# Two-megabyte weight transfers in slots of double size, with a new order of the first loads and of four routing copies

## The chip, the cores and the metric

The kernel runs on one core of a Trainium2 chip as one launch. The metric is device time in microseconds (us). Three runs of the kernel before gave a median of 1549.14 us (1548.66 to 1551.61).

## The reference

Two transformer blocks run one after the other on 256 tokens of width 1024, in float32:

```python
x = first_block(...)    # norm, w_in, pool mixer + attention, w_out; cross attention on mem; conv FFN
x = second_block(...)   # modulation by w_mod; latent attention over x and ctx; Fourier mix; w_out; experts

# the experts' part, the longest
logits = h @ w_router + b_router                 # 32 experts, the best 4 of each token
g = minimum(xb @ w_gate[e] + b_gate[e], 7)
u = clip(xb @ w_up[e] + b_up[e], -7, 7)
act = g * sigmoid(1.702 * g) * (u + 1)
y += gate * (act @ w_down[e] + b_down[e])
```

Each of w_gate, w_up and w_down is 32 matrices of 1024 x 1024 float32 (4 MB each), so the experts' weights are 384 MB; all other weights are 99 chunks of at most 1 MB.

## The kernel before

**The first 600 us.** All weights outside the experts lie in one array, `wall`, cut into 99 chunks of up to 128 x 2048 float32 (1 MB, a row of 8 KB in each partition). `load_chunk` (L372) takes a slot of the ring `ringA`, which has four slots of 1 MB, and issues the transfer on SyncE (SP). `convert_chunk` (L384) splits a chunk into a high part `wh` on ScalarE (ACT, L325) and a low part `wl` on VectorE (DVE, L326), in halves of 1024 columns; `wh` and `wl` have two buffers each. TensorE (PE) then runs three products for each weight (L432 to L434, or L439 to L441). The exception are the 24 chunks of `w_mod`: they are not split, and four matmuls read each straight from its slot (`mod_step`, L711). They are strewn as filler between the chunks of the FFN (and some earlier), in the order in which `emit` (L397) walks the list of items. `emit` loads up to four chunks ahead of the one in use; a transfer waits on SP until its slot's last reader is done, and SP issues in program order, so what stands behind a waiting transfer waits too.

**Small loads.** `vec` (the norms' weights), xT, `con`, `qkb` and others go by SP at the start. `mod_step` issues the bias row `brow` and the two rows `gate` on GpSimd (POOL) as soon as POOL comes to them, which for the first `brow` and both gates is at once.

**Routing.** `route_in(t)` (L1361) turns token half t with PE transposes and copies the two PSUM banks into `y`, a view of xT: the first half on ACT (L1369), the second on DVE (L1367). `route_mm` (L1382) then multiplies by the router's weights. In this stage the order on ACT and DVE is that of the code.

**The experts.** 384 transfers of 1 MB (128 rows of 8 KB) fill 20 slots: ringA's four, three further rings of 3, 4 and 8 that open as earlier pools close, and the place of xT. `load_to` (L1491) issues the next one as soon as the matmuls of L1615 or L1647 have read the slot. For each expert, `hidden` (L1602) runs 64 matmuls over w_gate and w_up and `project` (L1638) 32 over w_down, on blocks of 64 tokens; an expert with more than 64 tokens takes a second block through a branch (`extra`, L1659).

The lines that hold the sizes and the ring:

```python
RING_A = 4
RING_B = (3, 4, 8)
w = new(ring[0], [P, 2048], name="w")                          # load_chunk
w = new(rings[slots[i % len(slots)]], [P, 2048], name="w")     # load_to
```

Of the kernel before, what the change touches and what calls it, by code (L numbers as in the profile page):

```python
# [35 lines left out]
for _n, _w in (("mix_g", 8), ("xattn_g", 8), ("mem_g", 8), ("ffn_g", 8), ("pre_g", 8), ("pool_s", 4),  # L36
               ("xq_g", 2), ("xk_g", 2), ("ql_g", 3), ("kvl_g", 2), ("ffnpre_g", 8), ("cw0", 44),
               ("cw1", 44), ("cw2", 44), ("cb", 44)):
    VEC[_n] = _o
    _o += _w  # L40
NVEC = _o

# [108 lines left out]

RING_A = 4
RING_B = (3, 4, 8)
HL = 2
# [100 lines left out]
def network(ctx: ExitStack, tc: tile.TileContext, A):  # L255
# [27 lines left out]
    def here(shape, dt=F32, **kw):  # L283
        return new(pools["stage"], shape, dt, **kw)

    con = {"con": new(keep, [P, NCON["con"]], name="con")}
    vec = new(keep, [P, NVEC], name="vec")

# [7 lines left out]
    ident = C("ident", P)  # L296
    xT = new(ringx, [P, KD, T], name="xT", tag="w")

# [44 lines left out]
    con["conA"] = new(keep, [P, NCON["conA"]], name="conA", tag="k8a")  # L343
    qkb = new(keep, [P, 128 + NE], name="qkb")
    qkg = qkb[:, :128].rearrange("p (a b) -> p a b", a=2)
    brt = qkb[:, 128:]
    wrt = new(keep, [P, KD, NE], name="wrt")
    bexp = new(keep, [P, 512], name="bexp")
    cT = new(pools["tail"], [P, 8, 32], name="cT", bufs=1)
    wf = new(pools["tail"], [P, 2, P], name="wf", bufs=1)  # L350

# [45 lines left out]
    def emit():  # L397
        for n, (fn, w) in enumerate(prog.items):
            for key in w:
                where[key] = len(order)  # L400
                order.append(key)
        nl = nv = at = 0
        marks = {None}

        def convert_to(n):
            nonlocal nv
            while nv < min(n, nl):
                mark = prog.holds.get(order[nv][0])
                if mark not in marks and mark is not None:
                    return  # L410
                convert_chunk(nv)
                nv += 1

        for fn, w in prog.items:
            after = None
            if w:
                at = where[w[-1]]
            while nl < (len(order) if "out2" in marks else min(len(order), at + RING_A)) and prog.late.get(order[nl][0]) in marks:
# [277 lines left out]
    def mod_step(r, k):  # L696
        def fn(w):
            if r == 0 and k == 0:
                nc.scalar.activation(cT, cT, AF.Silu)
            if k == 0:  # L700
                S["mod"] = bank("g")
                S["brow"] = tmp512("brow", 1)
                nc.gpsimd.dma_start(S["brow"], A["bmod"][r])
                if r:
                    i = r - 1
                    S["gate", i] = new(keep if i else pools["tail"], [P, D], name="gate%d" % i, bufs=1)
                    nc.gpsimd.dma_start(S["gate", i], bass.AP(tensor=A["post"].tensor, offset=A["post"].offset + i * D,
                                                              ap=[[0, P], [1, D]]))
            ps = S["mod"]
# [650 lines left out]

    def route_in(t):  # L1361
        hT = y[:, t].rearrange("p (j q) -> p j q", j=KD)
        for half in range(2):
            ps = transposes(S["x4"][:, t], range(4 * half, 4 * half + 4))
            dst, src = hT[:, 4 * half:4 * half + 4], ps.rearrange("p (j q) -> p j q", j=4)
            if half:
# [66 lines left out]
    def out2_last(h):  # L1433
# [8 lines left out]
        def fn(w):  # L1442
# [9 lines left out]
            with tc.manual_schedule(engines={ACT, DVE}):  # L1452
# [29 lines left out]
    slots = ["b1"] * RING_B[0] + ["a"] * 2 + ["b2"] * RING_B[1] + ["a"] * (RING_A - 2) + ["b3"] * RING_B[2] + ["x"]  # L1482
    rings = {"a": ring[0], "x": ringx}

    def moe_open(name):
        n = int(name[1])
        rings[name] = ctx.enter_context(tc.tile_pool(name="ring" + name, bufs=RING_B[n - 1], side="left",
                                                     reuse_waits="tile"))
        load_to((RING_B[0] + 2, RING_B[0] + 2 + RING_B[1], len(slots))[n - 1])

    def load_to(n):  # L1491
        while state["n"] < min(n, len(seq)):
            i = state["n"]
            e, m, c = seq[i]
            w = new(rings[slots[i % len(slots)]], [P, 2048], name="w")
            if m < 2:
                src = A[("w_gate", "w_up")[m]][e].rearrange("(p j) n -> p (j n)", j=KD)
                src = src[:, 2048 * c:2048 * (c + 1)]
            else:
                src = A["w_down"][e].rearrange("(h p j) n -> h p (j n)", h=2, j=4)  # L1500
                src = src[c // 2][:, 2048 * (c % 2):2048 * (c % 2) + 2048]
            step = 1024 if i >= len(seq) - 1 else 2048
            for o in range(0, 2048, step):
                nc.sync.dma_start(w[:, o:o + step], src[:, o:o + step])
            chunk[e, m, c] = w.rearrange("p (j n) -> p j n", j=2)
            state["n"] += 1
# [95 lines left out]
    def hidden(e, xs, i, used=None):  # L1602
# [7 lines left out]
        for m, ps in enumerate(res):  # L1610
            for c in range(4):
# [5 lines left out]
                if used is not None:  # L1617
                    load_to(used + 4 * m + c + 1 + len(slots))
            if m == 0:
# [18 lines left out]
    def project(e, aT, swap=0, used=None):  # L1638

        po = pbank("t", 2)  # L1640
        for c in range(4):
# [7 lines left out]
            if used is not None:  # L1649
                load_to(used + 8 + c + 1 + len(slots))  # L1650
        return po
# [70 lines left out]
    gt, z = waiting  # L1722
    y = new(ringx, [P, 2, D], name="y", tag="w")
    for t in range(2):
# [64 lines left out]
```

## Time and profile before

| | |
|---|---|
| three runs, median | 1549.14 us (1548.66 to 1551.61) |
| the profiled execution | 1554.47 us, of which the span of the trace is 1552.5 us |
| PE busy | 1465.9 us, 94% of the span |
| DVE, ACT, POOL busy | 39%, 28%, 0% |
| mean DMA rate | 332 GB/s; about 425 GB/s from 650 us on |
| first matmul, first expert matmuls, end | 10.1 us, about 613 us, 1552.5 us |

The page gives, for each engine, the busy time and its share of the span, and the span in 40 slices of 38.8 us with a digit for the busy share. PEclk is the TensorE clock that was granted, in tenths of full speed. In the views, "PE", "DVE" and so on are engines, "PEld" is TensorE's weight load, "SPq" is SyncE's queue of DMA issues. A row of a timeline has its start, its length, the engine, the line, the operation and the tiles, and in brackets the idle time of the engine before it and what ended it.

### The profile page before, as it was taken

The numbers are of one execution on the slowest core, as the hardware profiler recorded it, in microseconds if no ns is written. First come the engines' busy times: TensorE is split into PE (matmuls) and PEld (weight loads), VectorE is DVE, ScalarE is ACT, GpSimd is POOL, SyncE is SP. The second block draws the span as 40 slices with busy tenths as digits, with TensorE's granted clock in tenths as the row PEclk, the third lists the DMA queues.
The fourth block names the chain that finished last, engine by engine and source line by source line (L and its number), as shares of the span: only waits on it lengthen the run. The fifth ranks groups of instructions, "written<-read, shape, count | busy, mean of one in ns | idle before, by whom it ended". The sixth has DMA issues, their size and how long they took to land. (4 is left out here: it accounts for less than half of the span.)

```text
span 1552.5 us, 20127 instructions
## 1 busy us (share of the span) xinstructions
PE 1465.9 (94%) x7985; PEld 831.0 (54%) x7985; DVE 603.9 (39%) x1436; ACT 431.3 (28%) x781; POOL 5.1 (0%) x13
## 2 busy tenths in 40 slices
PE   7999999999999998999999999999899999999996
PEld 5787888789998765333433333333334333333332
DVE  7859668666767465122212112112121122121113
ACT  5545655544547542111101111101111011011111
POOL 0000000000000000000000000000000000000000
PEclk9989999999999998999999999999999999999999
DMA  9645465886532448999999999999999999999993
GB/s 345 234 159 173 153 222 194 316 300 230 190 123 94 163 170 334 388 425 425 426 424 427 424 426 426 424 425 426 408 415 425 425 426 424 426 425 426 424 426 148
DMA packets 72883, 514.82 MB, mean 332 GB/s; under 512 B 8112, under 2 KB 8880, under 8 KB 11920
## 3 DMA queue, kind: packets, MB, share of 16 engines
q1 hardware_dynamic: 71712, 507.80, 80.8%
q0 software_dynamic: 1008, 4.78, 0.8%
q8 instruction: 110, 1.80, 0.4%
q14 instruction: 53, 0.43, 0.1%
HBM read 511.50 MB, written 1.05 MB: 330 GB/s over the span
## 5 line engine op out<-in xcount | busy, mean ns | idle before, releaser
L1615 PE MATMUL p_g<-w,xs 128*64 128x512 f32 x2112 | 461.1, 594 | 0.7 <-issue 0.7
L1615 PEld LDWEIGHTS p_g<-w,xs 128*64 128x64 f32 x2112 | 148.7, 137 | 310.8 <-issue 295.8
L1647 PE MATMUL p_t<-w,aT 128*64 128x512 f32 x1056 | 235.4, 598 | 2.2 <-ACT aT L1635 2.2
L326 DVE TENSOR_TENSOR wl<-w,wh 128x1024 fp32r<-128x1024 f32 (+3 forms) x150 | 173.1, 1178 | 50.2 <-ACT wh L325 50.0
L325 ACT ACTIVATE wh<-w 128x1024 fp32r<-128x1024 f32 (+3 forms) x150 | 146.8, 1016 | 132.9 <-issue 39.0
L1621 DVE TENSOR_SCALAR hg<-p_g 128x512 f32<-128x512 f32 x33 | 22.8, 692 | 378.9 <-PE p_g L1615 378.9
L1647 PEld LDWEIGHTS p_t<-w,aT 128*64 128x64 f32 x1056 | 73.2, 137 | 149.3 <-issue 130.1
L439 PE MATMUL ps_a<-wh,ah 128*128 128x512 f32 (+3 forms) x240 | 92.1, 387 | 12.7 <-ACT wh L325 11.1
L432 PE MATMUL ps_m<-ah,wh 128*128 128x256 f32 x352 | 101.6, 289 | 1.4 <-ACT wh L325 1.4
L1623 ACT ACTIVATE hs<-hg 128x512 f32<-128x512 f32 x33 | 20.8, 629 | 289.9 <-DVE hg L1621 289.9
L434 PE MATMUL ps_m<-ah,wl 128*128 128x256 f32 x352 | 100.4, 285 | 0.0
L433 PE MATMUL ps_m<-al,wh 128*128 128x256 f32 x352 | 100.4, 285 | 0.0
L1720 ACT ACTIVATE z<-p_t 64x512 f32<-64x512 f32 x63 | 37.3, 592 | 207.5 <-PE p_t L1647 207.1
L441 PE MATMUL ps_a<-wl,ah 128*128 128x512 f32 (+3 forms) x240 | 92.3, 385 | 0.0
L440 PE MATMUL ps_a<-wh,al 128*128 128x512 f32 (+3 forms) x240 | 91.8, 383 | 0.0
L1626 DVE TENSOR_SCALAR hu<-p_g 128x512 f32<-128x512 f32 x33 | 22.8, 692 | 154.7 <-PE p_g L1615 154.7
L1656 PE MATMUL p_y<-z,gt 128*128 128x512 f32 x128 | 63.9, 605 | 18.8 <-ACTq L1680 18.1
L1558 PE MATMUL p_t<-sel,x 128*128 128x128 f32 (+1 forms) x544 | 70.7, 285 | 11.2 <-ACT aT L1635 11.2
L1558 PEld LDWEIGHTS p_t<-sel,x 128*128 128x128 f32 x544 | 64.7, 195 | 28.6 <-issue 14.6
L1566 ACT ACTIVATE xs<-p_t,modT,A 128x128 f32<-128x128 f32 (+1 forms) x68 | 30.8, 453 | 158.9 <-PE p_t L1558 146.7
L432 PEld LDWEIGHTS ps_m<-ah,wh 128*128 128x128 f32 x352 | 68.1, 194 | 9.3 <-issue 3.4
L434 PEld LDWEIGHTS ps_m<-ah,wl 128*128 128x128 f32 x352 | 68.1, 194 | 2.4 <-DVE wl L326 0.8
(368 smaller groups left out, 1787.1 us busy)
## 6 DMA issues: line engine op xcount, KB each, us to landing
w<-w_gate_dram SPq DMA_DIRECT2D x128, 1024.0 KB, 19.6
w<-w_up_dram SPq DMA_DIRECT2D x128, 1024.0 KB, 19.5
w<-w_down_dram SPq DMA_DIRECT2D x127, 1024.0 KB, 19.6
w<-wall_dram SPq DMA_DIRECT2D x89, 1024.0 KB, 4.9
w<-wall_dram SPq DMA_DIRECT2D x4, 768.0 KB, 4.1
w<-wall_dram SPq DMA_DIRECT2D x3, 576.0 KB, 3.8
w<-wall_dram SPq DMA_DIRECT2D x2, 640.0 KB, 3.9
xT<-xT_dram SPq DMA_DIRECT2D x2, 512.0 KB, 7.7
```

Of the source, the lines that this page charges most:

```text
L325: nc.scalar.activation(hi, src, AF.Copy)
L326: nc.vector.tensor_tensor(lo, src, hi.bitcast(F32), op=ALU.subtract)
L432: nc.tensor.matmul(o, sh, mh, start=start, stop=False, **kw)
L433: nc.tensor.matmul(o, sh, ml, start=False, stop=False, **kw)
L434: nc.tensor.matmul(o, sl, mh, start=False, stop=stop, **kw)
L439: nc.tensor.matmul(o, a, wh, start=start, stop=False)
L440: nc.tensor.matmul(o, b, wh, start=False, stop=False)
L441: return nc.tensor.matmul(o, a, wl, start=False, stop=stop)
L1558: nc.tensor.matmul(ps[:, i * n * SLOTS:(i + 1) * n * SLOTS], x4[:, t, j * P:(j + 1) * P], sel[:, t].rearrange("p a b -> p (a b)"), start=t ...
L1615: last = nc.tensor.matmul(ps[64 * h:64 * h + 64, :], xs[:, 2 * c + jj, i * SLOTS:(i + 1) * SLOTS], w[:, jj, 512 * h:512 * h + 512], start= ...
L1647: nc.tensor.matmul(po[64 * h:64 * h + 64, :], s, w[:, jj, o:o + 512], start=c == 0 and jj == 0, stop=c == 3 and jj == 1)
L1656: nc.tensor.matmul(yb[t][h], gt[:, h, t * P:(t + 1) * P], z[:, h], start=False, stop=stop, skip_group_check=True)
```

## The change

Every ring slot becomes 128 x 4096 (2 MB), and there are half as many. An expert's matrix comes in two transfers of 2 MB (128 rows of 16 KB) in place of four; the last transfer of all is cut into four pieces. The chunks of `wall` remain transfers of 1 MB each, but two neighbours share a slot, which is taken when the even one is loaded. A pad of 16 floats and the move of `vec`, `qkb`, the router's weights, `wf` and the first gate into xT's (now double) slot bring all slots to addresses that are multiples of 256 bytes. At the start a tiny activation stands ahead of the data, xT comes in pieces of two, two and four k-rows around the halves of chunk 0, and `brow` and the gates are loaded by SP at later steps. In routing, ACT makes both copies of token half 0 and DVE both of half 1.

```diff
-RING_A = 4
-RING_B = (3, 4, 8)
+RING_A = 2
+RING_B = (1, 2, 4)
...
+    new(keep, [P, PAD], name="pad")
...
-    xT = new(ringx, [P, KD, T], name="xT", tag="w")
+    xw = new(ringx, [P, 4096], name="xT", tag="w")
...
+    xT = xw[:, :2048].rearrange("p (k t) -> p k t", k=KD)
+    vec = beside_x(NVEC)
...
+    first = new(pools["tail"], [P, 1], name="first", bufs=1)
+    nc.gpsimd.memset(first, 0.0)
+    nc.scalar.activation(first, first, AF.Identity)
     load(vec, A["vec"])()
-    load(xT[:, :4], A["xT"][:, :4])()
+    load(xT[:, :2], A["xT"][:, :2])()
...
-        w = new(ring[0], [P, 2048], name="w")
+        if i % 2 == 0:
+            S["w"] = new(ring[0], [P, 4096], name="w")
+        w = S["w"][:, 2048 * (i % 2):2048 * (i % 2) + 2048]
...
+            if i == 0 and o == 0:
+                load(xT[:, 2:4], A["xT"][:, 2:4])()
...
+            if k == 3 and r:
+                ...
+                load(S["gate", i], bass.AP(tensor=A["post"].tensor, offset=A["post"].offset + i * D, ap=[[0, P], [1, D]]))()
+            if k == 5:
                 S["brow"] = tmp512("brow", 1)
-                nc.gpsimd.dma_start(S["brow"], A["bmod"][r])
+                load(S["brow"], A["bmod"][r])()
...
-                route_in(0)
+                route_in(0, (ACT, ACT))
...
-                route_in(1)
+                route_in(1, (DVE, DVE))
...
-    seq = [(e, m, c) for e in experts for m in range(3) for c in range(4)]
+    seq = [(e, m, c) for e in experts for m in range(3) for c in (0, 2)]
...
-            w = new(rings[slots[i % len(slots)]], [P, 2048], name="w")
+            w = new(rings[slots[i % len(slots)]], [P, 4096], name="w")
...
-            step = 1024 if i >= len(seq) - 1 else 2048
+            step = 1024 if i >= len(seq) - 1 else 4096
```

The order of instructions on SP at the start, before and then after. In the kernel after, `vec` and `qkb` appear as parts of the tile xT.

```order
1 L353 DMA vec<-vec_dram 128x237
2 L353 DMA xT<-xT_dram 128x1024
3 L379 DMA w<-wall_dram 128x1024 x2
4 L353 DMA xT<-xT_dram 128x1024
5 L379 DMA w<-wall_dram 128x2048
6 L353 DMA con<-con_dram 128x480
```

```order
1 L365 DMA xT<-vec_dram 128x237
2 L365 DMA xT<-xT_dram 128x512
3 L396 DMA w<-wall_dram 128x1024
4 L365 DMA xT<-xT_dram 128x512
5 L396 DMA w<-wall_dram 128x1024
6 L365 DMA xT<-xT_dram 128x1024
7 L396 DMA w<-wall_dram 128x2048
```

The first half of chunk 0 now stands behind half as many bytes of xT, and POOL's three loads, which ran beside it, are gone from here.

SP in the stretch in which chunks of w_mod and of the FFN alternate, with what each transfer waits for (a name with DMAHW is the landing of an earlier transfer; DVE, PE and Activation are the readers of the slot), before and then after:

```order
67 L379 DMA w<-wall_dram 128x2048 [waits DMAHW7_49,DVE_49]
68 L379 DMA w<-wall_dram 128x2048 [waits DMAHW0_49,PE_49]
69 L379 DMA w<-wall_dram 128x2048 [waits DMAHW1_49,DVE_49]
70 L379 DMA w<-wall_dram 128x2048 [waits DMAHW2_49,PE_49]
71 L379 DMA w<-wall_dram 128x2048 [waits DMAHW3_49,PE_49]
72 L379 DMA w<-wall_dram 128x2048 [waits DMAHW4_49,DVE_49]
```

```order
68 L396 DMA w<-wall_dram 128x2048 [waits DMAHW0_49,DMAHW7_49,DVE_49,PE_49]
69 L396 DMA w<-wall_dram 128x2048
70 L396 DMA w<-wall_dram 128x2048 [waits DMAHW1_49,DMAHW2_49,DVE_49,PE_49]
71 L396 DMA w<-wall_dram 128x2048
72 L396 DMA w<-wall_dram 128x2048 [waits DMAHW3_49,DMAHW4_49,DVE_49,PE_49]
73 L396 DMA w<-wall_dram 128x2048
```

Where each transfer waited for the one reader of its own slot, the first of a pair now waits for the readers of both chunks that shared the slot, and the second follows it at once.

ACT in the first block between attention and `w_out`, where `pt` are the turned attention weights, `pooled` the pool mixer, and `ah` with ps_m its split, before and then after:

```order
35 L325 ACTIVATE wh<-w 128x1024
36 L652 ACTIVATE pt_689<-ps_m 128x4x128 x2
37 L325 ACTIVATE wh<-w 128x1024
38 L652 ACTIVATE pt_689<-ps_m 128x4x128
39 L681 ACTIVATE pooled<-ps_m 128x512
40 L636 ACTIVATE s_653,sm_s_660<-s_653,sm_b_658 128x256 x4
41 L325 ACTIVATE ah<-ps_a 128x512
42 L636 ACTIVATE s_674,sm_s_681<-s_674,sm_b_679 128x128 x4
43 L681 ACTIVATE pooled<-ps_m 128x512
44 L328 ACTIVATE ah<-ps_m,vec 128x256 x4
45 L652 ACTIVATE pt_755<-ps_m 128x4x128 x3
```

```order
37 L700 ACTIVATE pooled<-ps_m 128x512
38 L655 ACTIVATE s_667,sm_s_674<-s_667,sm_b_672 128x128 x4
39 L700 ACTIVATE pooled<-ps_m 128x512
40 L343 ACTIVATE ah<-ps_m,xT 128x256
41 L340 ACTIVATE wh<-w 128x1024
42 L343 ACTIVATE ah<-ps_m,xT 128x256 x2
43 L340 ACTIVATE wh<-w 128x1024
44 L671 ACTIVATE pt_748<-ps_m 128x4x128
45 L343 ACTIVATE ah<-ps_m,xT 128x256
46 L671 ACTIVATE pt_748<-ps_m 128x4x128 x2
```

Two halves of a chunk's conversion, `wh`, that stood ahead of the softmax now stand among the `ah` and `pt` behind it.

## Rows read from the trace of the kernel before

**Rows 1.** Page, part 2: PE's busy tenths in 40 slices (38.8 us each).
```profile
PE   7999999999999998999999999999899999999996
```

**Rows 2.** Windows: stretch, then length, busy by engine (count), clock, DMA share, GB/s.
```profile
250.00:300.00 50.00, 50.00 (x412) 44.58 (x410) 38.84 (x79) 29.51 (x51) 0.00 (x0) 1.00 0.62 232
300.00:350.00 50.00, 48.59 (x370) 39.04 (x367) 29.05 (x46) 19.11 (x28) 0.54 (x1) 1.00 0.81 296
650.00:1050.00 400.00, 384.15 (x1882) 148.16 (x1878) 77.52 (x180) 47.17 (x87) 0.00 (x0) 1.00 1.01 425
...
245.20:248.60 3.40, 3.40 (x17) 3.27 (x16) 3.40 (x12) 3.37 (x7) 0.00 (x0) 0.50 1.02 410
```

**Rows 3.** Timeline of the first 38 us: ACT's first work, PE's first matmul, one stall.
```profile
5.46 1.28 ACT L328 ACT_TABLE_LOAD   x1 [5.46 <-DMA xT<-xT_dram]
9.02 1.06 ACT L325 ACTIVATE wh<-w 128x1024 fp32r<-128x1024 f32 x1 [1.76 <-DMA w<-wall_dram]
...
10.13 0.79 PE L439 MATMUL ps_a<-wh,ah 128*128 128x512 f32 x1 [10.13 <-ACT wh L325]
...
37.02 0.47 PE L439 MATMUL ps_a<-wh,ah 128*128 128x512 f32 x1 [0.96 <-ACT wh L325]
```

**Rows 4.** DMA of the first 30 us: GB/s in 40 slices of 0.75 us.
```profile
GB/s 0 0 126 167 202 377 361 240 322 235 273 371 421 426 421 421 459 421 437 378 421 420 453 415 448 415 437 426 415 448 393 448 415 410 388 423 462 415 448 415
```

**Rows 5.** Timelines of ACT and PE, 69 to 81 us.
```profile
69.89 1.06 ACT L325 ACTIVATE wh<-w 128x1024 fp32r<-128x1024 f32 x1 [1.05 <-DMA w<-wall_dram]
...
71.81 1.06 ACT L325 ACTIVATE wh<-w 128x1024 fp32r<-128x1024 f32 x1
...
79.94 0.70 PE L690 MATMUL ps_m<-pooled,poolw 128*128 128x256 f32 x2 [2.44 <-ACT pooled L681]
```

**Rows 6.** Page, part 6: a transfer's KB and median us from issue to landing.
```profile
w<-wall_dram SPq DMA_DIRECT2D x89, 1024.0 KB, 4.9
```

**Rows 7.** Timeline of PE, 277 to 357 us: w_mod's matmuls (L711), next chunk's first (L432).
```profile
277.37 1.07 PE L711 MATMUL ps_g<-w,cT 128*32 128x512 f32 x8
...
284.31 1.92 PE L711 MATMUL ps_g<-w,cT 128*32 128x512 f32 x16
286.16 0.39 PE L432 MATMUL ps_m<-ah,wh 128*128 128x256 f32 x1
...
288.02 1.06 PE L711 MATMUL ps_g<-w,cT 128*32 128x512 f32 x8
...
340.30 1.06 PE L711 MATMUL ps_g<-w,cT 128*32 128x512 f32 x8
...
347.24 1.06 PE L711 MATMUL ps_g<-w,cT 128*32 128x512 f32 x8
348.24 0.38 PE L432 MATMUL ps_m<-ah,wh 128*128 128x256 f32 x1
...
356.04 0.39 PE L432 MATMUL ps_m<-ah,wh 128*128 128x256 f32 x1
```

**Rows 8.** Timeline of SP, 285 us, and lines by form, 262 to 362 us: conversions.
```profile
285.43 0.33 SPq L379 DMA_DIRECT2D w<-wall_dram  x1
...
L326 DVE TENSOR_TENSOR wl<-w,wh 128x1024 fp32r<-128x1024 f32 x27 | 32.7, 1222 | 14.3 <-ACT wh L325 14.3
...
L325 ACT ACTIVATE wh<-w 128x1024 fp32r<-128x1024 f32 x26 | 26.6, 1048 | 26.0 <-DMA w<-wall_dram 22.4 <-issue 3.6
```

**Rows 9.** Timeline of PE in routing, 594 to 601 us.
```profile
594.79 1.08 PE L1386 MATMUL ps_f<-wrt,xT 128*128 128x32 f32 x8 [1.61 <-DVE xT L1367]
...
597.41 3.62 PE L1386 MATMUL ps_g<-wrt,xT 128*128 128x32 f32 x16 [0.58 <-ACT xT L1369]
```

**Rows 10.** Last transfers and last products: SP's timeline, their landing, PE's timeline.
```profile
1502.58 10.12 SPq L1504 DMA_DIRECT2D w<-w_down_dram  x5
...
w<-w_down_dram SPq DMA_DIRECT2D x2, 512.0 KB, 17.7
...
1529.71 3.65 PE L1647 MATMUL p_t<-w,aT 128*64 128x512 f32 x16 [0.75 <-ACT aT L1635]
```

More of the change, by code (lines that the diff above doesn't have):

```diff
@@ L40 @@
     _o += _w
+PAD = 16
 NVEC = _o
@@ L284, in here @@
         return new(pools["stage"], shape, dt, **kw)
+    new(keep, [P, PAD], name="pad")
     con = {"con": new(keep, [P, NCON["con"]], name="con")}
-    vec = new(keep, [P, NVEC], name="vec")
     def C(name, n, off=0, rows=slice(None)):
@@ L296, in network, with beside_x @@
     ident = C("ident", P)
-    xT = new(ringx, [P, KD, T], name="xT", tag="w")
+    xw = new(ringx, [P, 4096], name="xT", tag="w")
+    at = 2048
+    def beside_x(n):
+        nonlocal at
+        at += n
+        return xw[:, at - n:at]
+    xT = xw[:, :2048].rearrange("p (k t) -> p k t", k=KD)
+    vec = beside_x(NVEC)
+    qkb = beside_x(128 + NE)
+    wrt = beside_x(KD * NE).rearrange("p (k e) -> p k e", k=KD)
+    wf = beside_x(2 * P).rearrange("p (k n) -> p k n", k=2)
+    gate0 = beside_x(D)
     def rsqrt(a, n, name, y=None):
@@ L417, in emit @@
                 at = where[w[-1]]
-            while nl < (len(order) if "out2" in marks else min(len(order), at + RING_A)) and prog.late.get(order[nl][0]) in marks:
+            while nl < (len(order) if "out2" in marks else min(len(order), at + 2 * RING_A)) and prog.late.get(order[nl][0]) in marks:
                 load_chunk(nl)
@@ L701, in fn @@
                 S["mod"] = bank("g")
-                S["brow"] = tmp512("brow", 1)
-                nc.gpsimd.dma_start(S["brow"], A["bmod"][r])
[L704 to L708, printed above, removed]
+            if k == 3 and r:
+                i = r - 1
+                S["gate", i] = new(keep, [P, D], name="gate1") if i else gate0
+                load(S["gate", i], bass.AP(tensor=A["post"].tensor, offset=A["post"].offset + i * D, ap=[[0, P], [1, D]]))()
+            if k == 5:
+                S["brow"] = tmp512("brow", 1)
+                load(S["brow"], A["bmod"][r])()
             ps = S["mod"]
@@ L1359, in mix_add, with route_in @@
             nc.vector.scalar_tensor_tensor(x4[:, t, c], y[:, t, c], r, x4[:, t, c], op0=ALU.mult, op1=ALU.add)
-    def route_in(t):
+    def route_in(t, engines):
         hT = y[:, t].rearrange("p (j q) -> p j q", j=KD)
@@ L1365, in route_in @@
             dst, src = hT[:, 4 * half:4 * half + 4], ps.rearrange("p (j q) -> p j q", j=4)
-            if half:
+            if engines[half] == DVE:
                 nc.vector.tensor_copy(dst, src)
@@ L1478, in network @@
     experts = [(e + NE // 2) % NE for e in range(NE)]
-    seq = [(e, m, c) for e in experts for m in range(3) for c in range(4)]
+    seq = [(e, m, c) for e in experts for m in range(3) for c in (0, 2)]
     chunk = {}
     state = {"n": 0}
-    slots = ["b1"] * RING_B[0] + ["a"] * 2 + ["b2"] * RING_B[1] + ["a"] * (RING_A - 2) + ["b3"] * RING_B[2] + ["x"]
+    slots = ["b1"] * RING_B[0] + ["a"] + ["b2"] * RING_B[1] + ["a"] + ["b3"] * RING_B[2] + ["x"]
     rings = {"a": ring[0], "x": ringx}
@@ L1488, in moe_open @@
                                                      reuse_waits="tile"))
-        load_to((RING_B[0] + 2, RING_B[0] + 2 + RING_B[1], len(slots))[n - 1])
+        load_to((RING_B[0] + 1, RING_B[0] + 1 + RING_B[1], len(slots))[n - 1])
     def load_to(n):
@@ L1494, in load_to @@
             e, m, c = seq[i]
-            w = new(rings[slots[i % len(slots)]], [P, 2048], name="w")
+            w = new(rings[slots[i % len(slots)]], [P, 4096], name="w")
             if m < 2:
                 src = A[("w_gate", "w_up")[m]][e].rearrange("(p j) n -> p (j n)", j=KD)
-                src = src[:, 2048 * c:2048 * (c + 1)]
+                src = src[:, 2048 * c:2048 * c + 4096]
             else:
                 src = A["w_down"][e].rearrange("(h p j) n -> h p (j n)", h=2, j=4)
-                src = src[c // 2][:, 2048 * (c % 2):2048 * (c % 2) + 2048]
-            step = 1024 if i >= len(seq) - 1 else 2048
-            for o in range(0, 2048, step):
+                src = src[c // 2]
+            step = 1024 if i >= len(seq) - 1 else 4096
+            for o in range(0, 4096, step):
                 nc.sync.dma_start(w[:, o:o + step], src[:, o:o + step])
-            chunk[e, m, c] = w.rearrange("p (j n) -> p j n", j=2)
+            for h in range(2):
+                chunk[e, m, c + h] = w[:, 2048 * h:2048 * h + 2048].rearrange("p (j n) -> p j n", j=2)
             state["n"] += 1
@@ L1617, in hidden @@
                 if used is not None:
-                    load_to(used + 4 * m + c + 1 + len(slots))
+                    load_to((used + 4 * m + c + 1) // 2 + len(slots))
             if m == 0:
@@ L1649, in project @@
             if used is not None:
-                load_to(used + 8 + c + 1 + len(slots))
+                load_to((used + 8 + c + 1) // 2 + len(slots))
         return po
@@ L1722, in network @@
     gt, z = waiting
-    y = new(ringx, [P, 2, D], name="y", tag="w")
+    y = new(ringx, [P, 4096], name="y", tag="w")[:, :2048].rearrange("p (t n) -> p t n", t=2)
     for t in range(2):
```

3 lines of the change are left out of this document (removed).

## The prediction

> **What bounds the kernel now.** I read the page's slices first: PE is busy nine tenths or more of nearly every slice; the exceptions are the first, the last and two between [rows 1]. So an edit pays only where PE waits, and costs where it makes PE wait. Then the windows by stage: from 650 us on PE is busy 384.15 of 400 us, and the DMA engines move 425 GB/s with a share of 1.01 [rows 2]. Both are full there, so I had to ask which ends last. The experts' 384 transfers of 1.0486 MB are 402.7 MB, or 947 us at 425 GB/s; PE goes through the experts in about 923 us (613 to 1536 us). The DMA is the slower of the two and lives on the 20 MB in the slots when PE starts. At the end there is little left of that lead: the last five issues end at 1502.58 + 10.12 = 1512.7 us, a piece of 512 KB lands 17.7 us after its issue, some 1530 us, and the last eighth of the products of w_down, for which it is meant, begins at 1529.71 + 7/8 x 3.65 = 1532.9 us [rows 10]. So PE bounds, by 2 to 3 us. Last I read the first 600 us for who waits for a transfer: the start, the stretch before w_out, and 262 to 362 us, where w_mod's chunks alternate with the FFN's.
>
> **The change part by part.** All durations come from the profiled execution, 1554.47 us, which is 5.3 us above the median of the three runs; a difference found in it is put on the median unchanged.
>
> *Experts' transfers.* 192 issues in place of 384, the same bytes. PE's order there stays as it was. A faster transfer gives nothing, since PE is the bound; a slot that comes free only when both its halves are read, and data that are whole only after 2 MB, cost up to one transfer's time, 1.0486 MB / 425 GB/s = 2.47 us of the lead, which the 2 to 3 us above just cover at the end, where the last pieces are 512 KB as before. I take 0; the row cost of 16 KB rows is not in this trace, and its price is with the rivals.
>
> *Start.* The first matmul starts at 10.13 us; it waits for ACT's split of the first half of chunk 0, which starts at 9.02 us when that half lands [rows 3]. Ahead of that half lie vec and xT's half, and POOL's three loads beside them (1.31 MB by their shapes). The slices of 0.75 us add up to (126 + 167 + 202 + 377 + 361) GB/s x 0.75 us = 0.92 MB by 5.25 us and 1.11 MB by 6.0 us [rows 4]. In the changed order vec (0.12 MB), xT's first quarter (0.26) and the half chunk (0.52) are 0.91 MB, with some of xT's second quarter beside them: they land between 5.3 and 6.1 us. The table load of 1.28 us, which now waits for xT until 5.46 us [rows 3], is done before. Two splits of xT and one square stand ahead of the weights' split on ACT, so it starts about 6.1 us, and PE at about 7.1: 3.0 us earlier. The stall of 0.96 us at 37.02 us, released by ACT [rows 3], should go as well, since the squares are now spread over the start. I take -4.0 us; the ends are -2 (the half lands 1 us later, the stall stays) and -5.
>
> *Attention to w_out.* Two halves of a conversion, of 1.06 us each, which ran at 69.89 and 71.81 us [rows 5], now stand among the splits and copies for which PE waits one by one; ahead of them PE already stands idle 2.44 us [rows 5]. They move because their chunk shares a slot with one that comes free late. Two of 1.06 less the overlap of some 0.1 each make +1.9 us; the ends are 0 (PE is held by DVE anyway) and +2.4, two low parts of 1.22 us on DVE [rows 8].
>
> *Chunks in pairs, 262 to 362 us.* This is the largest term. A transfer alone lands 4.9 us after its issue [rows 6]; issued as the second of a pair, 1.0486 MB later, 7.3. A pair is issued when the second chunk of the pair two before has been read. For a split chunk PE can begin 2.2 us after landing: a half on ACT, 1.05 us, and its low part on DVE, 1.22 us [rows 8], of which the first product needs only the high part. Then:
> - The pair whose slot w_mod frees at 277.37 + 1.07 = 278.4 us: its second chunk lands at 285.7 and is wanted at 286.16 [rows 7]; 0.4 us remain of 2.2, so 1.8 us late.
> - The pair freed by the first half of the block at 284.31 us, that is at 285.4: there the kernel before issues one transfer [rows 8], and its neighbour, a w_mod chunk, had gone 6.5 us earlier. Now that neighbour goes at 285.4, lands at 290.3, and L711 reads it straight at 288.02 [rows 7], with no conversion between: 2.2 us late. The delay so far moves the reader by 1.8 and the slot's release by 0.2 (an earlier pair of the same kind), so together the two make 2.4 us.
> - The pair freed at 340.30 + 1.06 = 341.4: its first lands at 346.2, wanted at 348.24 [rows 7], 2.0 of 2.2, so 0.2 late; two earlier pairs come out the same. The pair freed at 347.24 + 1.06 = 348.3: its second lands at 355.6, wanted at 356.04 [rows 7], so 1.8 late. Each of these is released after the delay before it, so they add: 3 x 0.2 + 1.8 = 2.4 us.
>
> Together +4.8 us. If a first product could go 1.1 us after landing (ACT's half alone), only 2.2 + 0.7 = 2.9 remain; with 2.9 us in place of 2.2 (DVE busy with the FFN's own work) it is 8.3.
>
> The Trainium skill, DMA: Bandwidth & Descriptors, section Anatomy of one DMA, gives a transfer a fixed cost of about 2.0 us and its bytes at 436 GB/s, for GpSimd's queue. By that 1 MB would land after some 4.4 us, the second of a pair after 6.8, and this term would shrink to about 2.9 us. The trace has 4.9 us for SP's transfers [rows 6], and the row decides.
>
> *Routing.* PE stands idle 1.61 us at 594.79 us for DVE's copy of half 0 [rows 9], which waits in DVE's order behind the norm. With both copies on ACT this wait goes; both copies of half 1 then follow each other on DVE, 0.7 us later than two engines side by side. The 1.61 us are not the end of the chain, since half 1 needs DVE's norm anyway. I take -0.5 us, with ends of -1.4 and +0.5.
>
> *Clock.* After a cluster of waits the granted clock falls: 3.4 us at 0.50 stand at 245.2 us [rows 2], which is 1.7 us lost. The stretch from 262 us on has none now [rows 2]. With stalls of about 2 us there I expect one: +1.7, ends 0 and +3.4.
>
> Sum: -4.0 + 1.9 + 4.8 - 0.5 + 1.7 = +3.9 us, 1558.4 us for a profiled execution and 1553.0 us for the median.
>
> **The rivals.**
> - *Slots in pairs cost nothing.* For it: PE now loses hardly anything to ACT's conversions though ACT waits 22.4 us for landings between 262 and 362 us [rows 8], and a long chain of readiness may hide 2 us. Against it: L711 at 288.02 us reads its chunk without a conversion. It leaves the start and the routing, -4.5 us: 1544.6, faster.
> - *Only the direct wait costs.* Conversions keep up, no clock falls: -4.0 + 1.9 + 2.9 - 0.5 = +0.3, 1549.4, no change.
> - *The experts become DMA-bound.* If rows of 16 KB move 1% slower, the 947 us grow by 9.5 us, of which the lead takes 2.9: +6.6 on top of the sum, 1559.6. It decides from 0.3% slower on. Against it: nothing in this trace has rows over 8 KB.
> - *The transfers gain.* The Trainium skill, DMA: Bandwidth & Descriptors, section Bandwidth, has 341 GB/s for 1 MB and 425 for 16 MB, so larger ones would be faster. The trace shows 425 with 1 MB already [rows 2], and PE is the bound: by this rival the experts' part does not move, and the time is that of the sum.
>
> **How the numbers follow.** Less than 0.2%, 3.1 us, can't be told from no change here. The forecast, 1553.0 with a range of its own of 1549.5 to 1558, has 0.47, of which 0.08 fall within 0.2%; the pairs that cost nothing 0.20, of which 0.17 are faster by over 0.2%; the direct wait alone 0.23, nearly all no change, 0.01 faster; the DMA-bound experts 0.10, slower. So faster 0.18, same 0.33, slower 0.49. The sum of the low ends, -5 + 0 + 2.9 - 1.4, is 1545.6; of the high ends, -2 + 2.4 + 8.3 + 0.5 + 3.4, it is 1561.7. The range is 1545 to 1560.
>
> **What would show it.** Right: the first matmul at about 7 us; an idle time of PE of about 2 us ahead of an L711 block near 290 us, released by a DMA, and further ones at 285 and 356 us released by ACT; the experts' first matmuls 3 to 5 us later than 613 us and as long as before. Wrong: PE's rows unbroken from 262 to 362 us, which makes the first rival; or a rate other than 425 GB/s from 650 us on together with PE waiting for a DMA, which makes the third.

## The result and the profile after

The changed kernel takes 1568.62 us (median of six runs, 1562.42 to 1572.90), the kernel before beside it 1550.96 us: ratio 1.0114, interval 1.0094 to 1.0134. Forecast were 1553.0 us and a range of 1545 to 1560: slower, as forecast, but beyond the range. The profiled execution took 1572.90 us (span 1571.0 us), 18.4 us more than that of before. Line numbers have moved: L432, L325 and L711 are now L451, L340 and L730, L1608 and L1615 are L1628 and L1635.

For "how late" I compare the k-th matmul of PE in the two traces; both kernels have 7985. In the changed kernel it starts 3.2 us earlier at 75 us (times of the kernel before), 1.7 us earlier at 77 us, 1.9 at 95 us, 2.0 earlier at 271 us, 12.1 later at 376 us, 11.0 at 588, 14.0 at 626 and to 860, 17.6 at 894 and 18.4 at the end. So 14.1 us, three quarters of the 18.4, arise between 271 and 376 us, where chunks of w_mod and of the FFN alternate.

The page's part 2, PE's busy tenths and the granted clock in tenths, in 40 slices of 39.3 us (PE of before: [rows 1]; PEclk of before has an 8 where a 7 stands here, and a 9 at the end):

```profile
PE   7999999999999998999999999999999999999996
PEclk9989999999999997999999999999999999999998
```

PE is as busy as before. Slices this wide do not show what happened; the windows do. Stretch, length, busy time of PE, PEld, DVE, ACT and POOL with counts, clock, DMA share, GB/s:

```profile
250.00:300.00 50.00, 47.30 (x357) 40.50 (x356) 34.91 (x66) 27.56 (x49) 0.00 (x0) 0.97 0.57 215
300.00:350.00 50.00, 48.15 (x350) 38.09 (x349) 27.10 (x42) 18.63 (x27) 0.00 (x0) 0.97 0.71 264
650.00:1050.00 400.00, 382.38 (x1848) 146.60 (x1844) 74.42 (x175) 46.02 (x85) 0.00 (x0) 0.99 1.00 425
...
290.80:294.20 3.40, 3.40 (x15) 2.98 (x15) 0.49 (x1) 1.58 (x2) 0.00 (x0) 0.50 1.01 426
314.70:318.10 3.40, 3.40 (x14) 2.96 (x14) 2.92 (x5) 0.58 (x2) 0.00 (x0) 0.50 0.94 349
365.90:372.70 6.80, 6.80 (x25) 5.29 (x25) 5.34 (x10) 2.74 (x4) 0.00 (x0) 0.50 0.99 393
881.30:884.70 3.40, 3.40 (x13) 0.58 (x9) 0.00 (x0) 0.00 (x0) 0.00 (x0) 0.50 1.01 429
```

In the first two rows PE's matmuls are 357 and 350, where before had 412 and 370 [rows 2]: it does less in the same time, partly idle, partly at half speed. In the last four the clock is at its lower level (1.2 GHz) from end to end, and PE counts as busy all through: what such a stretch costs, half its length, no busy row shows. In all of 250 to 350 us before had a clock of 1.00 [rows 2]. The experts' windows read alike: the changed kernel's 425 GB/s are 416 from 650 to 750 us and 429 behind it.

PE's waits from 262 to 385 us (start, length, line, tiles, and in brackets the idle time ahead and what ended it); in the kernel before the same blocks [rows 7] follow without an idle time, and the one wait of this stretch is the last line, at full clock and with no fall of the clock behind it:

```profile
276.73 0.39 PE L451 MATMUL ps_m<-ah,wh 128*128 128x256 f32 x1 [0.33 <-ACT wh L340]
290.07 1.22 PE L730 MATMUL ps_g<-w,cT 128*32 128x512 f32 x2 [2.37 <-DMA w<-wall_dram]
312.55 1.06 PE L730 MATMUL ps_g<-w,cT 128*32 128x512 f32 x8 [0.81 <-DVE mrow L734]
332.50 0.39 PE L453 MATMUL ps_m<-ah,wl 128*128 128x256 f32 x1 [0.28 <-DVE wl L341]
347.97 0.39 PE L451 MATMUL ps_a<-gh,wh 128*128 128x256 f32 x1 [0.71 <-ACT wh L340]
365.02 0.38 PE L451 MATMUL ps_m<-ah,wh 128*128 128x256 f32 x1 [1.94 <-ACT wh L340]
...
308.45 0.38 PE L432 MATMUL ps_m<-ah,wh 128*128 128x256 f32 x1 [1.41 <-ACT wh L325]
```

The two long ones are those of the forecast: a w_mod chunk read straight from its slot, forecast at 290 us and 2.2 us late (2.37 here), and the split chunk behind the last w_mod chunk, forecast 1.8 late (1.94 here). Behind each, 0.7 and 0.9 us after PE goes on, the clock falls: at 290.8 and at 365.9 us, the second time for 6.8 us. The third fall, at 314.7 us, stands 2.1 us behind the wait of 0.81 us.

Page, part 6, a transfer's KB and median us from issue to landing; before, a chunk landed in 4.9 us [rows 6]:

```profile
w<-wall_dram SPq DMA_DIRECT2D x89, 1024.0 KB, 6.6
```

As many chunks, of the same size, take 6.6 us in the median now, since the second of a pair queues behind the first: of two issued at 276.50 and 276.87 us one lands at 281.10 us, the other at 283.55.

**Time lost to the clock.** Every run comes with its span and mean clock. Span x clock is about the time it would take at full clock, span x (1 - clock) what it loses. Medians over the runs of each kernel:

| kernel | median us, ratio to before [interval] | at full clock | lost |
|---|---|---|---|
| before | 1549.4 to 1551.0 beside the others | 1528.2 to 1528.6 | 18.6 to 20.1 |
| changed | 1568.62, 1.0114 [1.0094, 1.0134] | 1533.3 | 32.9 |
| changed_again | 1570.31, 1.0125 [1.0100, 1.0150] | 1532.3 | 36.1 |
| start_only | 1544.16, 0.9956 [0.9937, 0.9976] | 1523.3 | 20.0 |
| shared_slots_only | 1563.42, 1.0096 [1.0070, 1.0121] | 1535.8 | 25.0 |
| shared_slots_exact | 1565.47, 1.0106 [1.0083, 1.0128] | 1538.3 | 25.0 |
| own_slots | 1547.64, 0.9982 [0.9962, 1.0001] | 1522.6 | 23.2 |
| own_slots_8k | 1547.74, 0.9978 [0.9969, 0.9988] | 1522.7 | 21.6 |
| own_slots_old_copies | 1548.76, 0.9991 [0.9980, 1.0002] | 1523.1 | 23.2 |
| experts_1mb | 1561.73, 1.0062 [1.0039, 1.0086] | 1532.0 | 28.1 |
| pairs_shifted | 1559.77, 1.0070 [1.0053, 1.0086] | 1531.3 | 25.7 |
| filled_wait | 1567.73, 1.0109 [1.0084, 1.0134] | 1536.8 | 29.0 |
| changed_code_moved | 1561.40, 1.0087 [1.0069, 1.0105] | 1531.2 | 28.1 |
| before_code_moved | 1552.92, 1.0020 [1.0005, 1.0035] | 1532.4 | 18.6 |

Among the runs of one kernel the column at full clock spans 2 to 6 us, the lost time 5 to 14. The change adds 5 us at full clock and loses 13 to 14 us more to the clock.

### The profile page after: what moved, and what is told of

Read it like the earlier page. It is cut to its first block, busy times and chain, and to the rows that moved or that the text cites. A ratio compares the mean times of both kernels' runs of the same rounds, so it can differ in the third digit from the quotient of the medians.

```text
span 1571.0 us, 19721 instructions
## 1 busy us (share of the span) xinstructions
PE 1479.9 (94%) x7985; PEld 839.5 (53%) x7985; DVE 605.0 (39%) x1436; ACT 431.8 (27%) x782; POOL 2.5 (0%) x9
## 5 line engine op out<-in xcount | busy, mean ns | idle before, releaser
L1635 PE MATMUL p_g<-w,xs 128*64 128x512 f32 x2112 | 461.7, 595 | 0.0
L1635 PEld LDWEIGHTS p_g<-w,xs 128*64 128x64 f32 x2112 | 150.2, 137 | 310.0 <-issue 307.8
L340 ACT ACTIVATE wh<-w 128x1024 fp32r<-128x1024 f32 (+3 forms) x150 | 146.6, 1016 | 128.9 <-issue 32.9
L451 PE MATMUL ps_m<-ah,wh 128*128 128x256 f32 x352 | 103.7, 295 | 2.3 <-ACT wh L340 2.3
L451 PEld LDWEIGHTS ps_m<-ah,wh 128*128 128x128 f32 x352 | 70.4, 200 | 10.0 <-ACT wh L340 6.5
```

The costliest lines, as they stand in the source:

```text
L340: nc.scalar.activation(hi, src, AF.Copy)
L451: nc.tensor.matmul(o, sh, mh, start=start, stop=False, **kw)
L1635: last = nc.tensor.matmul(ps[64 * h:64 * h + 64, :], xs[:, 2 * c + jj, i * SLOTS:(i + 1) * SLOTS], w[:, jj, 512 * h:512 * h + 512], start= ...
```

## Experiments

Theory: sharing slots in pairs makes PE wait in the first 600 us, and each wait of 2 us brings a fall of the clock that costs as much again. Rivals: the 2 MB transfers; the routing copies; the code's place in memory.

**One part undone: chunks of wall in slots of their own** (own_slots). The doubles of the experts stay, but those in ring A come as two tiles and two transfers of 1 MB.

```diff
-        if i % 2 == 0:
-            S["w"] = new(ring[0], [P, 4096], name="w")
-        w = S["w"][:, 2048 * (i % 2):2048 * (i % 2) + 2048]
+        w = new(ring[0], [P, 2048], name="w")
```

> The changed kernel with one thing undone: each chunk of wall has a slot of 1 MB of its own again (ring of four), and the two expert slots in that ring are filled by two transfers of 1 MB each; everything else as changed. Theory A (the shared slots cost the 14 us between 262 and 381 us and, by the new order of the last products of w_out, the 3 us in routing): 1546 to 1549 us, ratio to before 0.997 to 0.999, PE's rows unbroken from 262 to 362 us as before. Rival B (the 2 MB transfers of the experts cost): 1552 us or more. Rival C (the loads of brow and gate, now in SP's queue between the chunks, delay them): still 5 to 10 us slower than before.

0.9982 [0.9962, 1.0001], against 1.0114. The windows of its trace, columns as above:

```profile
262.00:300.00 38.00, 37.50 (x299) 30.83 (x300) 25.54 (x46) 20.24 (x34) 0.00 (x0) 1.00 0.82 314
300.00:385.00 85.00, 85.00 (x650) 73.97 (x649) 56.60 (x91) 36.99 (x54) 0.00 (x0) 0.98 0.69 259
650.00:1050.00 400.00, 382.81 (x1874) 148.67 (x1874) 76.89 (x183) 48.08 (x89) 0.00 (x0) 1.00 1.01 428
```

PE is unbroken from 300 to 385 us (half clock stands for 3.5 us at 300.7 us, behind a wait of 0.50 us), and its matmuls stay 8 to 12 us earlier than before from 95 us to the end. So the shared slots carry the whole loss. What is left of the change costs nothing; at full clock it gains 5.8 us, of which the clock takes some 3 to 5 back in the medians.

**The part alone** (shared_slots_only, shared_slots_exact): the kernel before with nothing but the shared slots. In shared_slots_only the last of the experts' transfers of ring A also go to a wrong half of a slot, so some products near the end read other weights; shared_slots_exact mends this.

```diff
-        w = new(ring[0], [P, 2048], name="w")
+        if i % 2 == 0:
+            S["w"] = new(ring[0], [P, 4096], name="w")
+        w = S["w"][:, 2048 * (i % 2):2048 * (i % 2) + 2048]
```

> The kernel before with one thing done: two neighbouring chunks of wall share a slot of 2 MB; the experts' transfers stay at 1 MB, first loads and routing as before. Theory A: 12 to 16 us slower than before (ratio 1.008 to 1.010), with PE idle about 2 us near 290 us ahead of a w_mod block and stretches of half clock behind it; no new order in routing, so 2 to 3 us less than the whole change. Rival B: within 2 us of before. Rival C: under 6 us slower.

> As shared_slots_only, where the place of one chunk of wall and that of an expert's piece were mixed up near the end; here each has its own. Theory A: the same, ratio to before 1.007 to 1.011, PE idle about 2 us near 290 us ahead of a w_mod block, and at 385 us 8 to 11 us behind the kernel before.

1.0096 and 1.0106, both nearly all of the changed kernel's loss, without its start and its large transfers. PE's long waits in shared_slots_exact:

```profile
291.34 1.04 PE L713 MATMUL ps_g<-w,cT 128*32 128x512 f32 x2 [2.38 <-DMA w<-wall_dram]
...
365.89 0.39 PE L434 MATMUL ps_m<-ah,wh 128*128 128x256 f32 x1 [2.14 <-ACT wh L325]
```

They are the two of the changed kernel. From 271 to 376 us its matmuls fall behind by 12.2 us, the changed kernel's by 14.1 and changed_again's by 10.3. Among the experts the lateness stays at 9.7 to 9.9 us: there the shared slots cost nothing.

**The other neighbours** (pairs_shifted): from chunk 36 on, each odd chunk shares with the even one behind it.

```diff
-        if i % 2 == 0:
+        odd = i > 36 and i % 2 == 0 or i < 36 and i % 2
+        if not odd:
```

> The changed kernel with the same shared slots, but from chunk 36 on other neighbours share: 36 stands alone, then 37 and 38, 39 and 40, and so on. By the arithmetic of the prediction (a pair goes when both chunks of the pair two before are read, lands 4.85 and 7.3 us later, and a split chunk is usable 2.2 us after landing) only 0.1 us at 293 us and 1.2 us at 308 us are late in place of eight late arrivals. Theory A (which chunks share a slot decides): 8 to 12 us faster than the changed kernel, ratio to before 1.000 to 1.004, no idle time of PE near 290 and 365 us. Rival C (any sharing costs, through SP's queue): as the changed kernel, 1.007 or more.

1.0070 [1.0053, 1.0086]: better than the changed kernel, but outside theory A's 1.000 to 1.004 and at the edge of rival C. From 271 to 376 us it falls behind by 2.9 us in place of 14.1, and no landing and no wait of over 0.2 us for a split stops PE there: its waits are 0.81 us for DVE's mrow and 0.15 us for a low part. So which chunks are neighbours decides in this stretch, as the working of the forecast had it. But the sharing isn't free elsewhere: at 239 us PE waits 1.80 us where the changed kernel waits 0.81, and falls back by 1.6 us between 200 and 250 us; at 577.6 us it waits 1.72 us for a split, a wait that the changed kernel does not have; and at 865 us it waits 2.18 us for its own sequencer, of which more below. The cost became smaller, and part of it moved.

**The start alone** (start_only): the tiny activation, xT in pieces, brow and gates on SP.

```diff
-    load(xT[:, :4], A["xT"][:, :4])()
+    load(xT[:, :2], A["xT"][:, :2])()
...
-                nc.gpsimd.dma_start(S["brow"], A["bmod"][r])
+                load(S["brow"], A["bmod"][r])()
```

> The kernel before with the new start alone: the tiny activation first, xT in pieces of two, two and four rows, brow and gates issued by SP at later steps. Theory A: 1.5 to 3.5 us faster than before (ratio 0.998), first matmul at about 8.5 us. Rival C: slower than before by 3 us or more, with delays between 262 and 362 us where brow and gate are loaded.

0.9956 [0.9937, 0.9976], more than expected: 6 to 7 us by the ratio, 5.1 us at full clock; its first matmul stands at 8.46 us. It beats both kernels.

**The transfers** (experts_1mb: shared slots kept, each double filled by two transfers of 1 MB; own_slots_8k: the same on top of own_slots).

```diff
-            step = 1024 if i >= len(seq) - 1 else 4096
+            step = 1024 if i >= len(seq) - 1 else 2048
```

> The changed kernel, but each double slot of the experts is filled by two transfers of 1 MB with rows of 8 KB. Theory A: as the changed kernel, ratio to before 1.009 to 1.013; the DMA rate falls back from 429 to about 425 GB/s from 650 us on and PE does not feel it. Rival B (rows of 16 KB or transfers of 2 MB cost PE time): 3 us or more faster than the changed kernel.

> As own_slots (chunks of wall in slots of their own), with the experts' data in transfers of 1 MB and rows of 8 KB. Theory A (large transfers neither cost nor give, since PE is the bound): within 1.5 us of own_slots, ratio to before 0.997 to 1.000. Rival B (transfers of 2 MB cost some 4 us, as the two runs with 1 MB suggest): 0.994 to 0.997.

own_slots_8k is own_slots to 0.1 us. In its trace the experts' window has 425 GB/s, in that of own_slots 428 (above): the transfers are faster with 16 KB rows, and PE does not feel it, 382.80 and 382.81 us busy. experts_1mb came out 9 us below changed_again and 7 below the changed kernel, which I had not expected, and which by the expectation of changed_again (below) speaks for rival B. At full clock the three are within 1.3 us. In the traces experts_1mb ends 10.9 us ahead of the changed kernel, and 8.3 of them stand at 500 us, ahead of the first transfer for the experts (530 us), where both kernels do the same: 3.3 come between 75 and 95 us, where the clock falls for 10.2 us in one and not in the other behind the same waits. Most of the difference is thus clock that the larger transfers cannot have cost; 3.6 us are one wait among the experts, of which more below.

**The copies** (own_slots_old_copies: own_slots with the routing copies as before).

```diff
-                route_in(0, (ACT, ACT))
+                route_in(0, (ACT, DVE))
...
-                route_in(1, (DVE, DVE))
+                route_in(1, (ACT, DVE))
```

> As own_slots, with the routing copies divided as in the kernel before (first half of each token half on ACT, second on DVE). If the new division gives the 0.5 us of the prediction: 0.3 to 1 us slower than own_slots (0.998 to 1.000). If it is the new division that costs own_slots its distance to start_only: 0.995 to 0.997.

1548.76 against 1547.64, and 0.5 us at full clock; the intervals overlap, so the times alone show nothing. Through routing (588 to 613 us of before) its matmuls move by +0.1 us, those of own_slots and of own_slots_8k by -0.5. By the traces the copies give about what was forecast, where routing's last chunk is on time.

**The changed kernel again** (changed_again), beside the others.

> The changed kernel itself once more, beside the others on one chip: theory A and its rivals alike 1.009 to 1.013. Against experts_1mb (1.0062) it tells whether the transfers of 2 MB cost: by theory A the two are equal within their intervals, by rival B 5 us or more apart.

1.0125, the same. In 271 to 376 us its matmuls fall behind by 10.3 us in place of 14.1: the two long waits are there (1.99 and 1.98 us), and the 0.81 us too, but no fall follows the last, and the one at 364.7 us takes 1.7 us in place of 3.4. So part of the cost comes with a run, not with the kernel.

**A wait filled** (filled_wait): four products of no use on PE behind the last w_mod chunk, ahead of the wait of 1.94 us.

```diff
+            if (r, k) == (2, 7):
+                with tc.issue_after(last.ins):
+                    keep_busy(4)
```

> The changed kernel with four idle products (ones by con, 480 columns, into a spare bank, read by nobody) put behind the last w_mod chunk, where PE stood idle 1.94 us at 365 us and the clock was at half for some 7 us after it; the wait for the chunk stays as long as it was. If the idle time itself brings the clock down: PE's idle time there falls under 0.5 us, the granted clock stays at 1.00 from 360 to 380 us, and the split's time comes back, 1.5 to 3.5 us less than the changed kernel at 385 us. If the clock falls for another reason (the time since the start, the earlier waits): half clock at 365 to 372 us as before.

1.0109, no better. The wait is gone, and the clock stays at 1.00 from 320 to 590 us. But the four products take 3.49 us: at 385 us the matmuls are 7.9 us late, 4.2 less than in the changed kernel and 0.4 more than in changed_again.

Does the fall at 365 us hang on the wait, then? All five traces that have a wait of 1.9 to 2.2 us there (the changed kernel, changed_again, experts_1mb and the two with shared slots alone) have a fall behind it, of 3.4 or 6.8 us. Of the nine without that wait seven have none, but two have one with no idle time of PE ahead of it, own_slots_8k (from 365.1 us, 6.8 us) and start_only (from 363.9, 3.4 us); their windows, columns as above:

```profile
360.00:370.00 10.00, 10.00 (x60) 9.11 (x59) 5.30 (x11) 2.76 (x4) 0.00 (x0) 0.75 0.28 103
...
360.00:370.00 10.00, 10.00 (x66) 9.11 (x66) 3.75 (x7) 2.00 (x2) 0.00 (x0) 0.83 0.33 110
```

So the wait brought the fall each time, but a fall can come without it, and what brings it then is not shown.

In filled_wait something new stands among the experts, where PE waits for its own sequencer:

```profile
1299.50 1.93 PE L1636 MATMUL p_g<-bexp,con 64*64 64x512 f32 x8 [2.13 <-PEq L1708]
...
1387.11 1.10 PE L1684 MATMUL p_y<-z,gt 128*128 128x512 f32 x2 [2.25 <-PEq L1708]
```

Each is behind a branch (L1708) and each comes with a stretch at half clock (3.4 us); the matmuls fall back by 3.9 and 3.0 us there. The changed kernel has one such wait, at another place:

```profile
881.02 1.98 PE L1628 MATMUL p_g<-bexp,con 64*64 64x512 f32 x8 [2.19 <-PEq L1700]
```

**The code moved** (changed_code_moved: two such products in place of four; before_code_moved: four in the kernel before).

> The changed kernel with two idle products behind the last chunk of w_mod, some 1.75 us of work in place of the wait of 1.94 us that PE has there for ACT's split (four of them took 3.49 us, and the granted clock stayed at full speed there). If only the filled wait counts, the lower clock at 360 to 371 us is gone at no cost, and PE's matmuls at 388 us stand 6.5 to 7.5 us earlier relative to the kernel before than the changed kernel's 14 (first run) or 7.5 (second run) less 3: between 4 and 8 us late. On the code: with four products the wait for PE's sequencer moved from 881 us to 1299 and 1387 us. If it is the place of the code, two products move it again, or remove it; if it is the larger transfers, one stands near 881 us as in the changed kernel. Time 0.998 to 1.003 of the changed kernel, 1.008 to 1.014 of the kernel before.

> The kernel before with four idle products put on PE behind the matmuls of the chunk of w_mod at 355 us, where PE has no wait; nothing else changes. They cost their own 3.5 us. In the trace of the kernel before the longest wait of PE for its own sequencer among the experts is 0.3 us; in the changed kernel one is 2.2 us (at 881 us), with the same matmuls and the same bytes. Theory 1, the place of the code: PE's instructions come in pieces of 16 KB, and a branch to an instruction of a piece that has not come waits; whether one does hangs on where the pieces end, which four more products move. Then one wait or more of 2.0 to 2.5 us for PE's sequencer may stand between 620 and 1536 us here too, at 1 MB transfers with rows of 8 KB, each with about 1.7 us lost to a lower granted clock. Theory 2, the larger transfers: an instruction piece comes late because it stands behind transfers of 2 MB. Then no such wait stands here, and the experts' matmuls are later by the same 3.5 us from first to last. A single trace without such a wait doesn't refute theory 1, since most places of the code need not have one.

The waits for the sequencer between 650 and 1530 us (total, count, longest) in changed_code_moved, then in before_code_moved:

```profile
PE p_g L1636 <- PEq L1708: 4.6, 15, 0.3
```

```profile
PE p_g L1616 <- PEq L1688: 4.7, 15, 0.4
```

With two products no wait is longer than 0.6 us. The same transfers thus come with one long wait, two or none, as the number of PE's instructions ahead differs: the place of the code decides where one stands. Both traces of the changed kernel have it behind the same branch (2.19 and 2.55 us). Whether it can happen with 1 MB transfers stays open: of the seven traces with 2 MB transfers four have one (the changed kernel, changed_again, pairs_shifted, filled_wait), of the seven with 1 MB none, the moved code of before included, nor experts_1mb, whose source differs from the changed kernel's in the transfers alone. So the larger transfers are not ruled out as a condition. before_code_moved (1.0020) settles neither of its theories: it has no long wait, and its experts' matmuls are not later by a constant 3.5 us but 2.4 to 3.5 us earlier than before's, through other falls of the clock. changed_code_moved has 1.0087, 4 us less than the changed kernel by the ratios (the intervals overlap), and its matmuls are 6.1 us late at 388 us, within the 4 to 8 expected; gone are 3.6 us at 881 us and 3.4 us of clock at 366 us, and the products cost about what they filled.

## Why the prediction was wrong in size

**Start, -4.0: right in size, by luck in part.** The first matmul starts at 8.48 us, 1.65 earlier; forecast were 3.0, to 7.1. ACT's split of the first weights starts at 7.38 us, when they land, not at 6.1: the half chunk lands later than the shapes gave. But the stall at 37 us [rows 3] went, and others before it: at 37 us PE is 3.2 us ahead, in changed_code_moved 4.5, in start_only 4.0. So stalls that were not in the sum gave what the first matmul did not. At full clock start_only gains 5.1 us.

**Attention to w_out, +1.9: right in the wait, without the clock behind it.** PE goes from 3.2 to 1.7 us ahead between 75 and 77 us, +1.5; in shared_slots_exact it is +1.9 to +2.2, in own_slots and start_only nothing. The two splits run at 77.43 and 79.23 us, among the `ah`, as the order had it. But the stretch goes on: from 75 to 95 us the changed kernel loses 1.3 us against before, while own_slots gains 4.5 and start_only 3.6. Half clock stands there for 10.2 us in before (from 81.4 us) and in the changed kernel (from 79.2), for 3.4 in start_only, and not at all in own_slots. The sum has no clock for this stretch; how much of it the sharing costs is not shown, since with the same two waits changed_code_moved has 6.8 us of it and experts_1mb none.

**Pairs, +4.8: right in mechanism, too small.** Of the 14.1 us, 6.8 are clock: half of 3.4 + 3.4 + 6.8 us. The other 7.3, half as much again as forecast, are waits and what hangs on them, within the ends of 2.9 and 8.3: six waits of 6.4 us in all, less the 1.41 us that before loses at 308.45 us. The two large waits came where and as long as the landing times of [rows 6] and 2.2 us for a split had them. Three things were not in the working: 0.81 us for DVE's mrow (in place of the 1.41 of before), 0.71 us at 347.97 us, and products that start some tenths late without a wait that the trace lists. One was too much: the split chunk of 286.16 us [rows 7], forecast 1.8 late, is taken up at 285.73 us with no idle time ahead of it; what the trace has in that block is 0.33 us, at 276.73.

**Clock, +1.7: the step that failed.** It counted one fall, and allowed two, and only for the stretch from 262 us. In that stretch there were three, 6.8 us. Over the whole trace half clock stands for 75.0 us, in before for 51.1, so the clock costs some 12 us of the 18.4; by the medians it is 13 to 14 us. I had priced a stall at its length and added the clock once, as a side effect of the cluster. In fact each of the two waits of 2 us is followed by a fall of its own, which costs 1.7 and 3.4 us: with the clock the waits of 2.37 and 1.94 us cost 1.7 and 2.8 times their length. That holds beyond this kernel: in the fourteen traces, between 20 and 1550 us, PE has 24 waits of 1.8 us or more outside the stretches that are at half clock already, and at every one the clock falls, at the latest 2.7 us behind it; of the 41 between 1.4 and 1.8 us 18 are followed by a fall. Falls without a wait ahead exist too (filled_wait, above). Why one fall lasts 3.4 us and another 6.8 or more, and why changed_again has fewer, was not settled.

**Routing, -0.5: wrong in sign, +2.9.** ACT's split of the last chunk in the changed kernel, and the squares (L1366) that end the products of token half 0 and of half 1:

```profile
593.59 2.01 ACT L340 ACTIVATE wh<-w 128x1024 fp32r<-128x1024 f32 x2 [1.96 <-DMA w<-wall_dram]
599.56 0.60 ACT L1366 ACTIVATE hsq<-ps_a 128x512 f32<-128x512 f32 x1 [3.96 <-PE ps_a L460]
...
601.89 0.60 ACT L1366 ACTIVATE hsq<-ps_a 128x512 f32<-128x512 f32 x1 [1.64 <-PE ps_a L460]
```

and PE behind them:

```profile
603.67 1.33 PE L557 MATMUL ps_m<-con,x 128*128 128x128 f32 x8 [1.88 <-DVE x L1378]
605.01 3.62 PE L1405 MATMUL ps_f<-xT 128*128 128x32 f32 x16
```

The last chunk's transfer goes out at 588.76 us, at 572.85 before: it too waits for a pair. Its split starts at 593.59 us, at 580.40 before. PE's order of products, which is fixed when the program is built, allows for that: half 1's over the chunk before the last now stand ahead of half 0's over the last one, where before half 0 was finished first. So the two squares stand 2.3 us apart, before 5.5 (585.36 and 590.87 us), and half 0's norm, 4 us on DVE (from 600.28 us), no longer lies beside half 1's products: PE waits 1.88 us for it ahead of the transposes, where before it did not wait. The wait of 1.61 us for the copy [rows 9] did go, so the waits come out about even; what is left is the clock, which is down for 20.5 us from 604.8 us, in before for 13.6 us from 596.8, some 3.4 us of loss. own_slots and pairs_shifted, whose last chunk comes earlier, have 13.6 to 13.7 too. I had costed the copies alone, and read the order of this stage by lines, where the exchange of two products of one line does not show. own_slots, whose last chunk comes on time, has the -0.5.

**Experts, 0: right on the transfers, and 4.4 us from elsewhere.** From 626 to 860 us PE keeps its 14.0 us, with 429 GB/s in place of 425 in the page's slices; the DMA-bound rival is out, and the gaining one is right in the rate and in that PE does not feel it. The Trainium skill, DMA: Bandwidth & Descriptors, section Bandwidth, has larger transfers faster, 341 GB/s for 1 MB and 425 for 16 MB, measured for GpSimd's queue; in direction the traces agree, by 1%, but a full queue of 1 MB already moves 425. Of the 4.4 us, 3.6 are the wait of 2.19 us at 881 us with its half of 3.4 us; this wait was in no rival. Another 1.7 are a fall of the clock from 1546.9 us on, and 0.4 come up to 1000 us; 1.3 are won back at 1124 us, where before stands still at full clock for a reason that its trace does not name.

**The rivals.** That pairs cost nothing is refuted by the waits above; it describes own_slots, where 1547.6 us stand beside its 1544.6. What was said for it, that PE now loses hardly anything to ACT's conversions, overlooked the wait of 1.41 us at 308.45 us, which the 48.59 of 50 us busy in [rows 2] already hold. That only the direct wait costs is refuted by the wait for a split at 365.02 us.

Sum of the profiled execution: -3.2 + 1.5 - 0.3 + 14.1 - 1.0 + 2.9 + 4.4 = 18.4 us, where -0.3 lies between 77 and 271 us and -1.0 between 376 and 588, where half clock stands for 10.3 us in before and for 6.8 in the changed kernel.

## What to carry to other kernels

Two transfers that share a slot make the earlier wait for the later one's reader; where chunks with and without a conversion alternate, the choice of neighbours decided here where PE stops and for how long, so follow each pair's release, landing and reader before you join slots, the stage's last chunk above all. In a kernel bound by PE, price a wait of 2 us at nearly twice its length, at times nearly three times, since here the clock fell behind each, and read span times clock beside the time. Undo one part at a time: here the start alone gains 0.4%, the transfers nothing, and the sharing lost more than both.

## What was not expected of the hardware

- Behind one wait of PE of about 2 us the lower clock stood for 3.4 us, once for 6.8 (at 290.8, 365.9 and 881.3 us); behind 0.81 us it did in one run of the changed kernel and not in the other, and in own_slots_8k and start_only it stood for 6.8 and 3.4 us near 364 us with no wait ahead.
- Which falls come differs from run to run of one kernel: the changed kernel lost between 25.0 and 37.7 us in six runs.
- Between 650 and 1530 us PE waits 2.1 to 2.6 us for its own sequencer behind a branch, at places that two or four more matmuls move or remove; else such a wait is 0.3 to 0.6 us.
- Rows of 16 KB in 2 MB move 428 to 429 GB/s, rows of 8 KB in 1 MB 425.
